# Five pairs of projections: a fixed order of their products, and the end of a head's attention one pair later

## The chip, the cores and the metric

The kernel runs on one core of one Trainium2 chip. The metric is the device time of one execution in microseconds, as a median of runs. The engines are named as the profile names them: PE is TensorE (matmuls; PEld its weight loads), DVE is VectorE, ACT is ScalarE, POOL is GpSimd, SP is SyncE, which here issues most of the DMAs. Each engine executes its instructions in the order in which the program has them.

## The reference

A decoder block for 512 tokens of width 2048. One projection gives two groups of heads: eight heads of 128 with compressed, selected and windowed attention (group A), and sixteen heads of 64 with a sliding window of 128 and a sink (group B). Each head's output is gated by a SiLU of a projected z. The output projection, the residual and an RMSNorm follow.

```python
def reference(x, w_in, ..., sinks, w_out, norm_g, final_g):
    h = _rmsnorm(x, norm_g[l])
    proj = h @ w_in[l]
    ...
    qb = _rope(_heads(qb, N_HEADS_B, HEAD_DIM_B)).reshape(B, S, N_KV_B, GROUP_B, HEAD_DIM_B)
    o_b = _banded_attention(qb, _rope(_heads(kb, N_KV_B, HEAD_DIM_B)), _heads(vb, N_KV_B, HEAD_DIM_B),
                            WIN_B, sink=sinks[l].reshape(N_KV_B, GROUP_B))
    y_b = o_b.reshape(B, S, WIDTH_B) * jax.nn.silu(zb)
    x = x + jnp.concatenate([y_a, y_b], axis=-1) @ w_out[l]
    return _rmsnorm(x, final_g)
```

## The kernel before

Everything is held in fp32, and each operand of a large matmul is split into a high and a low word: `unit` (L658) makes the high word by an ACT copy (L643) and the low word by a DVE subtraction (L644) of a 128x1024 quarter of weights, `raw`. A product's step is three matmuls, high by high, high by low and low by high (`mm3`, L126 to L129). There are three buffers for pairs of words.

The second group is worked through as eight "pairs" of 128 columns of q and 128 columns of z, h = 8 to 15. For h = 8 to 14 the function `pair` (L689) does not multiply the two 128-column blocks by x directly, but makes seven products of sums of quarters (a scheme of the Strassen kind) and combines them on DVE. Each product (`prod`, L668) is 8 steps, 24 matmuls of 128x128 by 128x256, into one half of a PSUM bank. A pair has two banks of 512 columns, `pa` and `pb`, out of a pool of two, so the next pair's `pb` is this pair's old `pa`. H0 and H1 are a bank's halves. In the order in which the code has them, the products are: "22" (pb H0), "p" (pa H0), "21" (pb H0, on top), "12" (pa H0, on top), "w" (pa H1), "u" (pb H1), "q" (pb H1, on top). Between them ACT copies halves out of the banks: 22's negated into `d` (L732), 21's into `zr` (L738), 12's into `qv` (`t1`, L747); DVE adds the rest with `plus` (L703).

The first pairs, h = 8 and 9, add quarters on DVE. In the five "wide" ones, h = 10 to 14, two quarters are summed while they are loaded: SP loads one (`load_quarter`, L686) and POOL issues a second load that accumulates onto it (L699). `tags` hands the buffers of a pair to the next in a rotated order.

The attention of the head whose q and z a pair has made (`attention`, from L880) is cut into jobs: s0 and s1 are scores and softmax of two parts (PE L900 and L901 into `spb`, DVE L904 to L908, ACT L909 to L918), k0 to k3 the transposes and values (PE L930 to L942, ACT L535 and L940), and `end` copies the result and gates it (`finish`, L512, which also stores it by a DMA). The loop at L947 hands these jobs as hooks to the next pair's products: `prod` calls them in the middle of the named product, and `behind_mm` (L663) keeps them behind the matmul issued last. Between these constraints, the order of the instructions on each engine is chosen by a scheduler, when the program is built, by its own estimate of times. After the loop, x is swapped in place for another copy (`swap_x`, L680), and `plain` makes the two 128-column blocks of h = 15 without the scheme.

## Time and profile before

| | |
|---|---|
| median of 3 runs | 826.99 us |
| lowest, highest | 824.44, 827.70 us |
| profiled execution | 826.69 us |
| its span, first to last instruction | 824.9 us |
| mean granted clock of PE | 0.999 |
| PE busy | 797.2 us |
| DVE busy | 685.4 us |

The span is the profiled execution's time from the first to the last instruction. The wide pairs lie between about 472 and 622 us of it. In rows in order of time, a number in brackets is the idle time of the engine just ahead of the instruction, with the instruction that the profile takes to have ended it. That name is inferred: where two instructions of an engine end close together, it can be the neighbour.

### The profile page before, as it was taken

What the parts mean: (1) busy time and instruction counts of PE and PEld (TensorE: products, weight loads), DVE (VectorE), ACT (ScalarE), POOL (GpSimd) and SP (SyncE); (2) the same over time, 40 slices, a digit from 0 to 9 for tenths busy, and PEclk for the clock granted to TensorE, in tenths of its full rate; (3) what the DMA queues carried; (4) which work ended last, traced back from release to release, by engine and by line L of the source; (5) the groups of instructions that cost most, each with busy time, mean ns of one, the idle gap of its engine ahead of it and who ended that gap; (6) DMA issues with size and microseconds to landing.
All of it is one profiled execution on the core that took longest, in us unless ns stands there. A gap on an engine that the chain in (4) does not pass through costs nothing.

```text
span 824.9 us, 15435 instructions
## 1 busy us (share of the span) xinstructions
PE 797.2 (97%) x5782; PEld 750.0 (91%) x5782; DVE 685.4 (83%) x1271; ACT 529.4 (64%) x1103; POOL 76.4 (9%) x69
## 2 busy tenths in 40 slices
PE   9999999999999999999999989999999999999996
PEld 8788898988999999999999989989888788999996
DVE  7869786865898989998898789989977588977895
ACT  6734456662677867868776568766866776553545
POOL 4500002012011011011010000000000000000000
PEclk9999999999999999999999999999999999999999
DMA  9655886899712314412321685656595336597835
GB/s 320 206 200 166 290 301 195 272 333 353 223 52 66 104 40 141 154 51 79 116 78 63 195 206 135 186 145 166 139 314 183 91 102 218 138 302 181 259 79 204
DMA packets 60954, 145.29 MB, mean 176 GB/s; under 512 B 6352, under 2 KB 19920, under 8 KB 60880
## 3 DMA queue, kind: packets, MB, share of 16 engines
q1 hardware_dynamic: 57424, 132.26, 48.7%
q0 software_dynamic: 3168, 11.54, 8.1%
q8 instruction: 45, 0.74, 0.4%
q10 hardware_dynamic: 288, 0.52, 0.2%
q14 instruction: 29, 0.24, 0.1%
HBM read 121.65 MB, written 20.55 MB: 172 GB/s over the span
## 4 chain that ended last, share of the span: by engine, by line
PE 75%; DVE 9%; ACT 6%; DMA 5%; issue 3%; POOL 1%; SPq 0%; DVEq 0%; ACTq 0%
PE pj L127 13%; PE pj L129 13%; PE pj L128 13%; PE oa L128 4%; PE oa L129 4%; PE oa L127 4%; PE bank L129 4%; PE bank L127 4%; PE bank L128 3%; PE sp L567 3%; DVE wlo L644 2%; DMA raw<-wq 2%; ACT whi L643 1%; DVE raw L703 1%; DMA xr<-xT 1%
## 5 line engine op out<-in xcount | busy, mean ns | idle before, releaser
L127 PE MATMUL pj<-xh,whi 128*128 128x256 f32 (+1 forms) x560 | 170.7, 305 | 8.7 <-DVE sums L907 2.6
L129 PE MATMUL pj<-xh,wlo 128*128 128x256 f32 (+1 forms) x560 | 170.1, 304 | 1.7 <-DVE wlo L644 1.7
L128 PE MATMUL pj<-xl,whi 128*128 128x256 f32 (+1 forms) x560 | 168.8, 301 | 0.0
L643 ACT ACTIVATE whi<-raw 128x1024 fp32r<-128x1024 f32 x98 | 103.0, 1054 | 55.3 <-PE pj L128 33.2
L644 DVE TENSOR_TENSOR wlo<-raw,whi 128x1024 fp32r<-128x1024 f32 x98 | 121.4, 1242 | 12.7 <-ACT whi L643 12.3
L127 PEld LDWEIGHTS pj<-xh,whi 128*128 128x128 f32 x560 | 105.4, 188 | 15.8 <-ACT whi L643 3.0
L129 PEld LDWEIGHTS pj<-xh,wlo 128*128 128x128 f32 x560 | 105.6, 189 | 7.0 <-DVE wlo L644 2.5
L128 PEld LDWEIGHTS pj<-xl,whi 128*128 128x128 f32 x560 | 105.4, 188 | 4.2
L97 DVE TENSOR_TENSOR wlo<-raw,whi 128x512 fp32r<-128x512 f32 (+2 forms) x74 | 81.3, 1104 | 33.5 <-ACT whi L96 33.0
L96 ACT ACTIVATE whi<-raw 128x1024 fp32r<-128x1024 f32 (+1 forms) x73 | 65.5, 901 | 53.1 <-PE pj L128 17.3
L127 PE MATMUL pj<-pu,whi 128*128 128x256 f32 x224 | 64.2, 287 | 2.9 <-DVE sums L908 1.5
L129 PE MATMUL pj<-pu,wlo 128*128 128x256 f32 x224 | 63.2, 282 | 0.5 <-DVE wlo L644 0.5
L128 PE MATMUL pj<-pu,whi 128*128 128x256 f32 x224 | 63.3, 283 | 0.0
L703 DVE TENSOR_TENSOR raw<-raw 128x1024 f32<-128x1024 f32 x46 | 59.1, 1285 | 0.2
L128 PE MATMUL oa<-wlo,xh 128*128 128x256 f32 (+1 forms) x168 | 50.9, 303 | 0.7 <-DVE wlo L1008 0.7
L127 PE MATMUL oa<-whi,xh 128*128 128x256 f32 (+1 forms) x168 | 50.4, 303 | 1.0 <-DVE sums L904 1.0
L129 PE MATMUL oa<-whi,xl 128*128 128x256 f32 (+1 forms) x168 | 50.3, 302 | 0.0
L127 PEld LDWEIGHTS pj<-pu,whi 128*128 128x128 f32 x224 | 42.3, 189 | 4.2 <-issue 1.6
L129 PEld LDWEIGHTS pj<-pu,wlo 128*128 128x128 f32 x224 | 42.3, 189 | 1.0 <-DVE wlo L644 0.9
L128 PEld LDWEIGHTS pj<-pu,whi 128*128 128x128 f32 x224 | 42.2, 188 | 0.0
L536 DVE TENSOR_TENSOR pl<-tp,ph 128x512 fp32r<-128x512 f32 x56 | 37.7, 683 | 4.9 <-ACT ph L535 4.8
L535 ACT ACTIVATE ph<-tp 128x512 fp32r<-128x512 f32 x56 | 32.1, 588 | 12.4 <-PE tp L930 8.4
(372 smaller groups left out, 2325.6 us busy)
## 6 DMA issues: line engine op xcount, KB each, us to landing
raw<-wq SPq DMA_DIRECT2D x65, 512.0 KB, 4.1
raw<-cw SPq DMA_DIRECT2D x16, 512.0 KB, 5.2
raw<-wos SPq DMA_DIRECT2D x15, 512.0 KB, 5.0
raw<-wq POOLq DMA_DIRECT2D x10, 512.0 KB, 5.5
rw<-wos SPq DMA_DIRECT2D x10, 512.0 KB, 5.2
xr<-xT SPq DMA_DIRECT2D x16, 256.0 KB, 5.1
raw<-w SPq DMA_DIRECT2D x8, 512.0 KB, 4.4
fd<-ft SPq DMA_DIRECT2D x4, 1024.0 KB, 6.0
```

What stands on the lines that cost most here:

```text
L96: last["hi"] = act.activation(hi[:, :width], rw[:, :width], AF.Copy).ins
L97: last["lo"] = dve.tensor_tensor(out=lo[:, :width], in0=rw[:, :width], in1=hi[:, :width].bitcast(F32), op=ALU.subtract).ins
L127: pe.matmul(ps, ah, bh, start=first, stop=False, skip_group_check=go_on)
L128: pe.matmul(ps, ah, bl, start=False, stop=False, skip_group_check=go_on)
L129: recent["mm"] = pe.matmul(ps, al, bh, start=False, stop=last, skip_group_check=go_on).ins
L535: act.activation(ph, tp, AF.Copy)
L536: dve.tensor_tensor(out=pl, in0=tp, in1=ph.bitcast(F32), op=ALU.subtract)
L567: pe.matmul(sp[:, a:b], qq[:, qs], kk[0][:, ko:ko + b - a], start=pi == 0, stop=pi == 2)
L643: act.activation(hi, src, AF.Copy)
L644: last["lo"] = dve.tensor_tensor(out=lo, in0=src, in1=hi.bitcast(F32), op=ALU.subtract).ins
L703: return dve.tensor_tensor(out=out, in0=a, in1=b, op=op).ins
```

## The change

`prod` gets a flag, `in_turn`, by which all matmuls of a product are kept behind the last matmul of the product before. The hooks are now called after the whole product has been written down, but still stand behind the matmul of its middle. `pair` keeps only h = 8 and 9. The five wide pairs get a function of their own, `wide_pair`, which prescribes the order 22, p, 21, 12, u, w, q: with u ahead of w, each product goes into the other bank than the one before it, and so does the next pair's 22, which follows q. The words of u are made ahead of those of w; `d` takes u first and w second. The buffers rotate in another way: the next pair's sum quarter takes the buffer of this pair's x3. In the loop, k0 moves from u to q, and k2, k3, k1 and `end` of a head no longer stand in q, or behind it, of the pair that does its scores, but in "p" of the pair after it; after the loop, in the plain product's third step.

```diff
-    def prod(bank, u, op, new, hooks=None):
-        for m in range(8):
...
-            if m == 3:
-                behind_mm((hooks or {}).get(op, ()))
+    def prod(bank, u, op, new, hooks=None, in_turn=False):
+        with ExitStack() as behind:
+            if in_turn:
+                behind.enter_context(tc.issue_after(last["prod"]))
+            for m in range(8):
...
+                if m == 3:
+                    mid = recent["mm"]
+        last["prod"] = recent["mm"]
+        recent["mm"] = mid
+        behind_mm((hooks or {}).get(op, ()))
+        recent["mm"] = last["prod"]
...
-            c1, c2, c5, c3, c4 = tags
-            tags[:] = c4, c1, c2, c3, c5
...
+    def wide_pair(h, hooks):
...
+        def do(bank, u, op, new):
+            prod(bank, u, op, new, hooks, True)
+
+        c1, c2, c5, c3, c4 = tags
+        tags[:] = c2, c1, c3, c4, c5
...
+        do(pb[:, H0], u0, "22", True)
+        act.activation(d, pb[:, H0], AF.Copy, scale=-1.0)
+        x3 = load(c3, 1)
+        do(pa[:, H0], u3, "p", True)
+        plus(d, d, pa[:, H0])
+        u2 = unit(x3)
+        do(pb[:, H0], u2, "21", False)
+        act.activation(zr[:, H1], pb[:, H0], AF.Copy)
+        u4 = unit(sm)
+        x4 = load(c4, 2, 3)
+        plus(sm, sm, x1)
+        plus(jj, d, zr[:, H1])
+        do(pa[:, H0], u4, "12", False)
+        act.activation(qv[:, H0], pa[:, H0], AF.Copy)
+        u5 = unit(sm)
+        plus(sm, sm, x3)
+        plus(jj, jj, qv[:, H0], ALU.subtract)
+        do(pb[:, H1], u5, "u", True)
+        plus(d, d, pb[:, H1])
+        u1 = unit(x4)
+        do(pa[:, H1], u1, "w", True)
+        plus(qv[:, H1], d, pa[:, H1])
...
+        u6 = unit(sm)
+        do(pb[:, H1], u6, "q", False)
+        plus(jj, jj, pb[:, H1])
+        plus(zr, zr, rstdb, ALU.mult)
...
-    held = None
+    held, tail = None, []
     for i in range(7):
-        hooks = {}
+        hooks = {"p": tail}
         if held:
             j, end, _ = held
-            hooks = {"12": [j["s0"]], "w": [j["s1"]], "u": [j["k0"]], "q": [j["k2"], j["k3"]], "end": [j["k1"], end]}
-        q2, st = pair(8 + i, (), hooks)
+            hooks.update({"12": [j["s0"]], "w": [j["s1"]], "q": [j["k0"]]})
+            tail = [j["k2"], j["k3"], j["k1"], end]
+        q2, st = wide_pair(8 + i, hooks) if i > 1 else pair(8 + i, (), hooks)
...
-    qp = plain(15, 0, {7: [j["s0"]], 11: [j["s1"]]})
+    qp = plain(15, 0, {2: tail, 7: [j["s0"]], 11: [j["s1"]]})
```

What this makes of the order on two engines is shown at three places. The first is PE where pair 12 begins, with the numbers of the buffers: `pj_6123` is the `pa` of pair 11 and `pj_6481` the `pb` of pair 12 (one bank), `xh`, `xl` are the words of x.

```order
L127 MATMUL pj_6123<-xh_108,whi_6289 128x256
L128 MATMUL pj_6123<-xl_109,whi_6289 128x256
L129 MATMUL pj_6123<-xh_108,wlo_6290 128x256
L127 MATMUL pj_6481<-xh_108,whi_6487 128x256
L128 MATMUL pj_6481<-xl_109,whi_6487 128x256
```

The next pair's 22 stood directly behind w of the same bank. In the changed kernel `pj_6084` is the `pb` of pair 11 and `pj_6441` the `pb` of pair 12, and `KH1`, `KL1` are operands of q:

```order
L127 MATMUL pj_6084<-KH1_123,whi_6393 128x256
L128 MATMUL pj_6084<-KL1_125,whi_6393 128x256
L129 MATMUL pj_6084<-KH1_123,wlo_6394 128x256
L127 MATMUL pj_6441<-xh_108,whi_6447 128x256
L128 MATMUL pj_6441<-xl_109,whi_6447 128x256
```

Now q, in the other bank, stands ahead of it.

The second place is ACT between the copies of 21 (L738) and 12 (L747) of pair 12; `whi` are splits into words, `ttb` with `sums` the softmax (L912 exponentials), `ph`, `pd` and `ob` copies for values.

```order
L738 ACTIVATE zr_6483<-pj_6481 128x256
L643 ACTIVATE whi_6705<-raw_6497 128x1024
L940 ACTIVATE pd_6439<-tp_6436 128x256
L535 ACTIVATE ph_6461<-tp_6456 128x512
L643 ACTIVATE whi_6764<-raw_6497 128x1024
L912 ACTIVATE ttb_6603,sums_6602<-ttb_6603,sums_6602 128x128
L949 ACTIVATE ob_6469<-opb_6365 64x512
L912 ACTIVATE ttb_6603,sums_6602<-ttb_6603,sums_6602 128x128
L909 ACTIVATE sums_6602<-sums_6602 128x4
L912 ACTIVATE ttb_6611,sums_6602<-ttb_6611,sums_6602 128x256 x2
L747 ACTIVATE t1_6482<-pj_6480 128x256
```

In the changed kernel the same two copies are L793 and L799, and L963 the exponentials:

```order
L643 ACTIVATE whi_6676<-raw_6585 128x1024
L793 ACTIVATE zr_6443<-pj_6441 128x256
L643 ACTIVATE whi_6750<-raw_6457 128x1024
L799 ACTIVATE t1_6442<-pj_6440 128x256
L535 ACTIVATE ph_6516<-tp_6511 128x512
L991 ACTIVATE pd_6527<-tp_6524 128x256
L643 ACTIVATE whi_6804<-raw_6802 128x1024
L963 ACTIVATE ttb_6615,sums_6614<-ttb_6615,sums_6614 128x128 x2
```

The two copies now stand one split apart, both ahead of the exponentials; before, that of 12 stood behind four of them.

The third place is ACT in pair 14 of the changed kernel (L969 are the softmax's normalisations, L819 the tanh of the gate).

```order
L643 ACTIVATE whi_7359<-raw_7171 128x1024
L643 ACTIVATE whi_7390<-raw_7299 128x1024
L969 ACTIVATE ttb_7062<-ttb_7062,sums_7061 128x256 x2
L969 ACTIVATE ttb_7070<-ttb_7070,sums_7061 128x256 x2
L819 ACTIVATE st_7151<-zr_6800 128x512
L799 ACTIVATE t1_7156<-pj_7154 128x256
L535 ACTIVATE ph_7230<-tp_7225 128x512
L991 ACTIVATE pd_7241<-tp_7238 128x256
L643 ACTIVATE whi_7464<-raw_7171 128x1024
L535 ACTIVATE ph_7250<-tp_7245 128x512
L793 ACTIVATE zr_7157<-pj_7155 128x256
L963 ACTIVATE ttb_7329,sums_7328<-ttb_7329,sums_7328 128x128 x2
```

Here the copy of 21 (L793) stands last, behind the copy of 12, a split and three copies for values.

## Rows read from the trace of the kernel before

**Rows 1.** Page part 1: engine, busy us, share of the span, instructions.
```profile
PE 797.2 (97%) x5782; PEld 750.0 (91%) x5782; DVE 685.4 (83%) x1271; ACT 529.4 (64%) x1103; POOL 76.4 (9%) x69
```

**Rows 2.** Table by stretches, one a pair; columns as in its second line.
```profile
core 0: us, PE busy (x) PEld busy (x) DVE busy (x) ACT busy (x) POOL busy (x), PEclk, DMA share, GB/s
528.91:557.35 28.44, 26.27 (x219) 25.32 (x219) 24.59 (x54) 21.48 (x50) 1.83 (x3) 1.00 0.59 145
557.35:583.58 26.23, 24.92 (x210) 24.44 (x211) 24.22 (x54) 18.04 (x41) 1.73 (x2) 1.00 0.61 165
583.58:611.80 28.22, 26.39 (x218) 25.40 (x218) 24.60 (x52) 20.89 (x49) 0.00 (x0) 1.00 0.71 210
```

**Rows 3.** PE in time: start us, us, instruction, idle before it, releaser.
```profile
479.78 0.36 PE L127 MATMUL pj<-pu,whi 128*128 128x256 f32 x1 [1.46 <-DVE sums L908]
...
484.64 0.38 PE L127 MATMUL pj<-xh,whi 128*128 128x256 f32 x1 [1.36 <-ACT dd L732]
...
502.57 0.39 PE L129 MATMUL pj<-xh,wlo 128*128 128x256 f32 x1 [0.24 <-DVE wlo L644]
...
528.91 0.36 PE L127 MATMUL pj<-xh,whi 128*128 128x256 f32 x1 [1.31 <-DVE sums L907]
...
542.23 0.38 PE L127 MATMUL pj<-pu,whi 128*128 128x256 f32 x1 [0.34 <-ACT whi L643]
...
551.99 0.39 PE L127 MATMUL pj<-xh,whi 128*128 128x256 f32 x1 [0.96 <-ACT t L747]
...
557.35 0.38 PE L127 MATMUL pj<-xh,whi 128*128 128x256 f32 x1 [0.87 <-DVE dd L703]
...
583.58 0.36 PE L127 MATMUL pj<-xh,whi 128*128 128x256 f32 x1 [1.31 <-DVE sums L907]
...
597.59 0.38 PE L127 MATMUL pj<-pu,whi 128*128 128x256 f32 x1 [0.47 <-ACT whi L643]
...
606.90 0.39 PE L127 MATMUL pj<-xh,whi 128*128 128x256 f32 x1 [0.95 <-ACT t L747]
...
611.80 0.50 PE L127 MATMUL pj<-xh,whi 128*128 128x512 f32 x1 [0.42 <-DVE dd L703]
```

**Rows 4.** VectorE in time, the additions that read w's half.
```profile
528.35 0.41 DVE L703 TENSOR_TENSOR dd<-dd,pj 128x256 f32<-128x256 f32 x1
...
556.88 0.41 DVE L703 TENSOR_TENSOR dd<-dd,pj 128x256 f32<-128x256 f32 x1
```

**Rows 5.** ScalarE in time, ahead of and at the copy of 12's half.
```profile
551.34 0.19 ACT L912 ACTIVATION_READ_ACCUMULATOR ttb<-ttb,sums 128x1 f32 x1
551.55 0.38 ACT L747 ACTIVATE t<-pj 128x256 f32<-128x256 f32 x1
```

**Rows 6.** Load chain of pair 10's sum quarter: SP, GpSimd and ScalarE in time.
```profile
472.45 0.61 SPq L686 DMA_DIRECT2D raw<-wq  x1
...
479.92 0.90 POOL L699 DMA_DIRECT2D raw<-wq  x1 [6.36 <-DMA raw<-wq]
...
485.48 1.06 ACT L643 ACTIVATE whi<-raw 128x1024 fp32r<-128x1024 f32 x1 [0.90 <-DMA raw<-wq]
```

**Rows 7.** ScalarE by line, 528.91 to 583.58: busy us, mean ns, idle before.
```profile
L643 ACT ACTIVATE whi<-raw 128x1024 fp32r<-128x1024 f32 x14 | 14.8, 1054 | 10.2 <-PE pj L128 9.4 <-ACT sums L909 0.8
...
L535 ACT ACTIVATE ph<-tp 128x512 fp32r<-128x512 f32 x6 | 3.5, 588 | 0.8 <-PE tp L930 0.8
...
L747 ACT ACTIVATE t<-pj 128x256 f32<-128x256 f32 x2 | 0.8, 384 | 0.0
```

**Rows 8.** Page part 6: DMA issues, count, KB each, median us to landing.
```profile
raw<-wq SPq DMA_DIRECT2D x65, 512.0 KB, 4.1
...
raw<-wq POOLq DMA_DIRECT2D x10, 512.0 KB, 5.5
```

**Rows 9.** DMA issues in 600 to 626, columns as in rows 8.
```profile
xh<-xd SPq DMA_DIRECT2D x2, 512.0 KB, 7.8
```

**Rows 10.** PE in time: w's last matmul, and the plain product's second half.
```profile
610.66 0.28 PE L129 MATMUL pj<-xh,wlo 128*128 128x256 f32 x1
...
621.35 0.40 PE L127 MATMUL pj<-xh,whi 128*128 128x512 f32 x1
```

More of the change, by code (lines that the diff above doesn't have):

```diff
@@ L666, in behind_mm @@
                 job()
[L668 to L674 removed]
+    def prod(bank, u, op, new, hooks=None, in_turn=False):
[3 more added lines that the diff above has]
+            for m in range(8):
+                cs = slice(m * P, m * P + P)
+                ah, al = xf[op, m]
+                mm3(bank, u[0][:, cs], u[1][:, cs], ah, al, new and m == 0, m == 7, not new)
+                if m == 3:
[4 more added lines that the diff above has]
+        recent["mm"] = last["prod"]
     def swap_x(source):
@@ L691, in pair, with load @@
         early = list(early)
-        wide = h > 9
-        def load(tag, quarter, other=None):
-            if early:
-                return early.pop(0)
-            t = load_quarter(src, tag, quarter)
-            if other is not None:
-                pool.dma_start(t, src[other], accum_op=ALU.add)
-            return t
+        def load(tag, quarter):
+            return early.pop(0) if early else load_quarter(src, tag, quarter)
         def plus(out, a, b, op=ALU.add):
             return dve.tensor_tensor(out=out, in0=a, in1=b, op=op).ins
-        if wide:
-            c1, c2, c5, c3, c4 = tags
-            tags[:] = c4, c1, c2, c3, c5
-        else:
-            c1, c2, c4, c3 = tags
-            tags[:] = (c4, c1, c3, c2) if h < 9 else (c4, c1, "raw4", c3, c2)
+        c1, c2, c4, c3 = tags
+        tags[:] = (c4, c1, c3, c2) if h < 9 else (c4, c1, "raw4", c3, c2)
         pa, pb = [psp.tile([P, S], F32, name="pj", tag="pj") for e in range(2)]
@@ L715, in pair @@
         d, jj = qv[:, H1], zr[:, H0]
-        if wide:
-            d = wb.tile([P, 256], F32, name="dd", tag="dd")
         x1 = load(c1, 3)
@@ L721, in pair @@
         u3 = unit(x2)
-        if wide:
-            sm = load(c5, 0, 2)
-        else:
-            sm = x2
-            x4 = load(c4, 2)
-            with ExitStack() as behind:
-                if "jj" in last:
-                    behind.enter_context(tc.issue_after(last["jj"]))
-                plus(x2, x2, x4)
+        sm = x2
+        x4 = load(c4, 2)
+        with ExitStack() as behind:
+            if "jj" in last:
+                behind.enter_context(tc.issue_after(last["jj"]))
+            plus(x2, x2, x4)
         prod(pb[:, H0], u0, "22", True, hooks)
@@ L740, in pair @@
         u4 = unit(sm)
-        if wide:
-            x4 = load(c4, 2, 3)
-        else:
-            plus(x4, x4, x1)
+        plus(x4, x4, x1)
         plus(sm, sm, x1)
@@ L764, in pair, with load, plus @@
         plus(jj, jj, pb[:, H1])
-        behind_mm((hooks or {}).get("end", ()))
         last["jj"] = plus(zr, zr, rstdb, ALU.mult)
+        st = wk.tile([P, S], F32, name="st", tag="st")
+        act.activation(st, zr, AF.Tanh, scale=0.5)
+        dve.scalar_tensor_tensor(out=st, in0=st, scalar=1.0, in1=zr, op0=ALU.add, op1=ALU.mult)
+        return qq, st
+    def wide_pair(h, hooks):
+        src = wq[h - FIRST]
+        def load(tag, quarter, other=None):
+            t = load_quarter(src, tag, quarter)
+            if other is not None:
+                pool.dma_start(t, src[other], accum_op=ALU.add)
+            return t
+        def plus(out, a, b, op=ALU.add):
+            return dve.tensor_tensor(out=out, in0=a, in1=b, op=op).ins
+        def do(bank, u, op, new):
+            prod(bank, u, op, new, hooks, True)
+        c1, c2, c5, c3, c4 = tags
+        tags[:] = c2, c1, c3, c4, c5
+        pa, pb = [psp.tile([P, S], F32, name="pj", tag="pj") for e in range(2)]
+        qv = wk.tile([P, S], F32, name="t1", tag="t1", bufs=1)
+        zr = wk.tile([P, S], F32, name="zr", tag="xr", bufs=1)
+        d, jj = wb.tile([P, 256], F32, name="dd", tag="dd"), zr[:, H0]
+        x1 = load(c1, 3)
+        u0 = unit(x1)
+        x2 = load(c2, 0)
+        u3 = unit(x2)
+        sm = load(c5, 0, 2)
+        do(pb[:, H0], u0, "22", True)
[20 more added lines that the diff above has]
+        plus(qv[:, H1], d, pa[:, H1])
+        t2 = wk.tile([P, S], F32, name="t2", tag="t2", bufs=1)
+        for a, b in ((0, 64), (64, 0)):
+            dve.tensor_tensor(out=t2[a:a + 64], in0=qv[b:b + 64], in1=sinA[b:b + 64], op=ALU.mult)
+        dve.tensor_tensor(out=qv, in0=qv, in1=cosA, op=ALU.mult)
+        dve.tensor_tensor(out=qv, in0=qv, in1=t2, op=ALU.add)
+        qq = qb_split(qv)
+        u6 = unit(sm)
+        do(pb[:, H1], u6, "q", False)
+        plus(jj, jj, pb[:, H1])
+        plus(zr, zr, rstdb, ALU.mult)
```

3 lines of the change are left out of this document (removed).

## Prediction

> **What bounds the kernel now.** I read the engines' shares first: PE is busy 797.2 us and DVE 685.4 us [rows 1], in a span of 824.9 us. PE is the engine that is hardly ever idle, so only what removes an idle stretch of PE can shorten the run by itself; nothing in this change removes matmuls. The second view is the table by stretches, one row for each of three wide pairs [rows 2]. The reader is to see two things there: PE is idle for 1.3 to 2.2 us in each pair (28.44 less 26.27, 26.23 less 24.92, 28.22 less 26.39), and DVE is busy 24.2 to 24.6 us in each, that is, at most 1.8 us below PE. ACT, with 18.0 to 21.5 us, has more room on the whole, but it works in order as well. So the gain has a floor that is near: if PE loses its gaps, a pair takes some 25 us, and DVE fills nearly all of that.
>
> The third view is PE in order of time, and from it the rows with an idle stretch ahead of them, from the first of pair 10 to the first of the plain product that follows pair 14 [rows 3]. These are all that are over 0.2 us: eleven, in sum 9.69 us. They fall into four kinds. (a) The first product of the next pair, "22", stands directly behind "w", whose half lies in the same bank: 1.31, 0.87 and 1.31 us, and 0.42 us where the plain product stands there, 3.91 us together. The releaser's name "sums L907" is that of the neighbour; what really ends just ahead is the DVE addition of the half that w has written (it starts at 528.35 and lasts 0.41 us, PE goes on at 528.91; at 556.88 with 0.41 us, PE at 557.35) [rows 4]. (b) "w" waits for ACT's copy of "12" out of the other half of its own bank, 0.96 and 0.95 us; the copy started at 551.55 and lasted 0.38 us, w started at 551.99 [rows 5]. (c) Words that come late: 0.24, 0.34 and 0.47 us. (d) The two of pair 10, 1.46 and 1.36 us.
>
> **The change part by part.** *q between w and the next 22.* PE then has the 24 matmuls of q, and 8 score products, ahead of the 22 that waits for DVE's reading of w. A matmul takes about 24.92 us / 210 = 0.119 us of PE's time [rows 2], so q alone covers 2.8 us against waits of 0.87 to 1.31 us. All of kind (a) goes: -3.91 us. What is late next there is q's own words: their raw sum is the last of three additions on DVE, and the old order had q even later, without a wait, so I put that at 0; if the cover failed the 22's wait would come back, up to 1.31 us a pair.
>
> *12, scores, u, w.* PE's order of these three is as before; what moves is ACT's. The copy of 12 now stands ahead of the next softmax's exponentials and not behind them, so (b) goes: -1.91 us. (c) goes with it, since u's words are now made ahead of w's: -1.05 us. Together what can be had behind pair 10 is 6.87 us.
>
> *Pair 10.* Its gaps I leave in the sum. The words of its 12 come at the end of a serial chain: the load issued at 472.45, the accumulating load behind it at 479.92, ACT's split at 485.48 [rows 6]. 12 cannot start earlier than this, and the chain is not touched. If PE were sooner at 12 by 2.82 us it would wait there. Between 0 and 0.5 us may be had; I take 0.
>
> *What the new order adds.* u goes into the bank into which 21 went, and both orders need 21's copy by ACT first. Before, that copy had long been done. Now it is queued on ACT behind the splits of two further words and four normalisations. A split takes 1.05 us, a copy of a half 0.38 us and a copy of transposed weights 0.59 us [rows 7]. Following ACT's queue with these through pairs 11 to 13, the copy ends 0.1 to 0.4 us after PE is ready for u: 0.25 us each, +0.75 us. In pair 14 it is worse: behind the copy of 12 stand a copy of transposed weights (0.59), a smaller one (0.38 as a half), a split (1.05), another copy of weights (0.59) and only then the copy for u (0.38), 3.0 us, while PE has only 8 score products and 11 transposes and values, 19 times 0.119 us = 2.3 us at most, part of them ahead of ACT's start. The wait there is between 0 (the queue runs ahead) and 2.5 us (the normalisations ahead of it run late as well). The nearest row is the wait for ACT's copy in the same pair before, 0.95 us [rows 3]; I take 1.0 us. In pairs 12 and 13 the copy of 22's half stands behind the two copies that make the rotated queries, and 21 waits for it: 0 to 0.7 us, I take 0.35 each, +0.7 us. Sum of the additions: +2.45 us.
>
> A rule speaks against counting the neighbours alone. By the rows the wait is for the bank, not for the bytes: w writes one half and waits for the copy of the other [rows 3, 5]. The Trainium skill, "PSUM — Partial Sum Buffer", section "PSUM bank collisions raise a hardware error", says that a different address in the same bank and quadrant still collides, and asks for semaphores by bank. By it u waits for ACT's copy of 21 though a whole product lies between them, and w for the copy of 12: a prescribed order of products does not take that dependence away, only the time of ACT's queue does. The rows agree with it. If ACT kept its old place for these copies the two waits would be gone, and the sum would be 2.45 us lower.
>
> *The tail of the head before, in "p" of the next pair.* The same instructions, about 5 us later on PE and off the path: values, additions and one store. On SP the store and on ACT the copies stand behind the next pair's first splits; who waits for them is the output stage after 650 us. Cost 0; bounds -0.3 to +0.5 us a pair, by the copies' 0.38 to 0.59 us [rows 7], if they stand ahead of a split that PE needs.
>
> *Buffers.* The sum quarter's accumulating load now takes the buffer of x3 and is issued only when the last raw addition has read it, late in the pair. From there to ACT's split of it I count some 16 us. A load lands after 4.1 us and an accumulating one after 5.5 us [rows 8], 9.6 us serially, so it is hidden; pair 10's chain took 13.0 us (472.45 to 485.48) [rows 6] and would be hidden as well. Cost 0, slack 3 to 6 us.
>
> *The end of the stretch.* The swap of x into the odd places goes out when w has ended, as before. The loads of it land after 7.8 us [rows 9]. Before, the second half of the plain product that needs it began 10.7 us after w's last matmul (621.35 against 610.66) [rows 10], since q lay inside it; now q lies ahead of all of it, and the need comes some 9.9 us after w. 0 to 1 us, I take 0.
>
> The sum is -6.87 + 2.45 = -4.4 us. The profiled execution took 826.69 us (1.8 us around its span), which is 0.3 us under the median of 826.99 us; the difference is applied to the median: **822.6 us**.
>
> **Rivals.** *All waits go.* ACT runs ahead of its queue and the additions are 0: -6.87 us, 820.1 us. For it: ACT is idle some 7 to 8 us in a pair [rows 2]. Against: it must be idle at the right time, and its order is fixed.
>
> *The wait moves.* With PE's order fixed, one late word stops everything behind it, where before PE's queue had an attention piece or another product in between. DVE needs 24.6 us of the 25 that are left, and ACT's queue holds copies that PE waits for. If each of four pairs loses 1.5 us in this way (kinds a and b came to 1.3 to 1.8 us a pair), then -6.87 + 6 is about -1: 826 us. DVE's share speaks for it.
>
> The Trainium skill, "Perfetto Trace Analysis", section "Identifying the Most-Contended Engine", has matmul busy time as a poor measure and the weight loads' as a better one. The weight loads are busy 24.44 us where matmuls show 24.92 [rows 2]; by that PE has half a microsecond more room in a pair, and DVE would be the bound by 24.2 against 24.4, nearly a tie, which speaks for this rival a little.
>
> *Slower: the sum quarter comes late.* One mechanism: its buffer is free later, so two serial transfers start later. It decides when the two together exceed 16 us. Were both twice as long as now (8.2 + 11.0 = 19.2 us), each of four pairs would wait 3.2 us: -4.4 + 12.8 gives 835 us. Against: the longest chain seen is 13.0 us.
>
> *The change does not do what it says.* If PE's effective order were much as before, the time stays: 827 us. The order written down in the program speaks against it.
>
> **How the numbers follow.** Chances: forecast 0.44 (821 to 824.3), all waits go 0.20 (818 to 821), the wait moves 0.22 (824.3 to 828), sum quarter late 0.09 (over 831), no effect 0.05. About 0.5% is what a measurement of this kernel can tell from no change, that is 4.1 us: faster means under 822.9. The forecast's own range lies on both sides of that: 0.27 under, 0.17 within. Faster 0.27 + 0.20 = 0.47; same 0.17 + 0.22 + 0.04 = 0.43; slower 0.09 + 0.01 = 0.10. The range leaves out the sum quarter's case and the outer end of "all waits go", and takes in the bounds of the unknown costs: 818.0 to 828.0.
>
> **What would show it.** Right: no idle stretch ahead of a pair's 22; none ahead of w; small ones, released by ACT's copy, ahead of u, the largest in pair 14; the pairs 11 to 14 some 25.2 us long; pair 10 as before. Wrong: idle of PE behind DVE's splits in every pair (the wait moved), a wait of ACT for the accumulating load ahead of 12 (sum quarter late), or a pause in the middle of the plain product (swap late).

## The result, and the profile after

The change makes the kernel slower: 833.58 us against 828.87 us (medians of 7 runs each, 4.7 us apart). The ratio on record, over all runs, is 1.0069 [1.0041 to 1.0096], by which the loss is some 5.7 us. The forecast was 822.6 us. One execution of i1 below, 839.17 us, is over 1.5% above the fastest of its kernel and is left out of its median.

| | before | after |
|---|---|---|
| profiled execution, us | 826.69 | 831.98 |
| its span, us | 824.9 | 830.2 |
| granted clock of TensorE, mean | 0.999 | 0.994 |
| PE idle in the span, us | 27.7 | 30.0 |

The first part of the page, as in [rows 1], and the shares of the chain that ended last:

```profile
PE 800.2 (96%) x5782; PEld 752.1 (91%) x5782; DVE 683.7 (82%) x1271; ACT 529.6 (64%) x1103; POOL 76.9 (9%) x69
...
PE 71%; DVE 11%; ACT 8%; DMA 6%; issue 3%; SPq 0%; POOL 0%; DVEq 0%; ACTq 0%
```

In these two profiles the loss has two parts, and the first line shows both. The same 5782 matmuls are busy 3.0 us longer (800.2 against 797.2), and PE is idle 2.3 us more (830.2 less 800.2 against 824.9 less 797.2). The chain's share of PE, 75% before, is 71%: more of it runs through waits on other engines.

PE in order of time, the rows with a longer idle stretch ahead of them, from pair 10 to the output stage (start us, us, instruction, idle before it and its releaser; in a block of columns of that stage that is made by seven products the first is called p, the second 22):

```profile
487.74 0.39 PE L127 MATMUL pj<-xh,whi 128*128 128x256 f32 x1 [1.93 <-ACT whi L643]
...
513.45 0.38 PE L127 MATMUL pj<-xh,whi 128*128 128x256 f32 x1 [0.90 <-ACT dd L787]
...
540.49 0.38 PE L127 MATMUL pj<-xh,whi 128*128 128x256 f32 x1 [1.59 <-ACT dd L787]
...
566.64 0.38 PE L127 MATMUL pj<-xh,whi 128*128 128x256 f32 x1 [0.22 <-ACT dd L787]
...
599.11 0.36 PE L951 MATMUL spb<-VH,qs 128*128 128x256 f32 x1 [1.54 <-DMA qs<-qlo]
...
603.51 0.38 PE L127 MATMUL pj<-pu,whi 128*128 128x256 f32 x1 [1.05 <-ACT zr L793]
...
702.63 0.39 PE L127 MATMUL oa<-whi,xh 128*128 128x256 f32 x1 [2.63 <-ACT whi L1059]
...
731.90 0.38 PE L127 MATMUL oa<-whi,xh 128*128 128x256 f32 x1 [1.15 <-ACT whi L1059]
```

Set beside [rows 3], none of the eleven gaps is left in its place: no row ahead of a pair's 22, none ahead of w. In their stead stand fewer and longer ones: 12 of pair 10 (1.93), 21 of pairs 11 to 13 (0.90, 1.59, 0.22), the scores in pair 14 (1.54), u of pair 14 (1.05), and two in the output stage (2.63, 1.15), where the longest before was 0.69.

The table by stretches, columns as in [rows 2]: pairs 11, 12 and 13, and then two short stretches directly behind a wait, in pair 10 and in the output stage.

```profile
506.29:532.64 26.35, 25.45 (x216) 24.91 (x215) 24.49 (x54) 19.72 (x45) 1.73 (x2) 1.00 0.67 170
532.64:559.72 27.08, 25.49 (x217) 24.95 (x216) 24.04 (x55) 21.11 (x49) 1.74 (x2) 1.00 0.65 161
559.72:585.20 25.48, 25.26 (x217) 24.64 (x216) 23.93 (x53) 19.67 (x45) 1.74 (x2) 1.00 0.60 156
488.40:491.80 3.40, 2.93 (x15) 2.87 (x15) 3.18 (x5) 3.19 (x7) 0.00 (x0) 0.51 0.23 35
703.50:706.80 3.30, 3.30 (x17) 3.30 (x17) 3.30 (x6) 2.22 (x4) 0.00 (x0) 0.50 0.53 169
```

The pairs are 25.5 to 27.1 us long, PE idle 0.2 to 1.6 us in each. In the two short stretches the granted clock is 0.51 and 0.50, the lower of the two levels (1.2 GHz): in the second, matmuls start 0.21 us apart (703.61 to 706.81), right behind it 0.11 us. Each stretch costs at most 1.7 us, its length by one less the clock; what is called lost by the clock below is counted so, and is a bound from above, since PE also waits in part of some stretches. In the profile of before the clock is full from the first pair to the last microseconds. Its mean, 0.999, is the highest that any execution of that kernel shows; the 22 beside h0 below have 0.993 to 0.999, so a part of this difference is the choice of the execution.

Set against before, the 5.3 us of span come out so. PE is 1.3 us late at 457 us already, in front of the change (the idle there varied by more than a microsecond between profiles, and is no effect of it). From there to the first product of the output stage, at 655.34 us (654.12 before), it wins 1.6 us of idle time (9.0 against 10.65 us) and loses 1.7 us by the clock behind the wait of pair 10: nothing is won. From there to the end it takes 4.1 us more, with 2.6 us more of waits and 1.7 us by the clock in the stretch shown, and that stage's code isn't touched by the change.

**The output stage.** What the scheduler did there is seen on ScalarE, VectorE and SyncE, at the end of head 15, three answers in this order:

```profile
686.33 0.60 ACT L1000 ACTIVATE ob<-opb 64x512 f32<-64x512 f32 x1 [4.50 <-PE opb L988]
687.48 1.06 ACT L1059 ACTIVATE whi<-raw 128x1024 fp32r<-128x1024 f32 x1 [0.55 <-PE pj L129]
688.57 0.59 ACT L1000 ACTIVATE ob<-opb 64x512 f32<-64x512 f32 x1
...
686.96 0.68 DVE L1001 TENSOR_TENSOR ob<-opb,ob 64x512 f32<-64x512 f32 x1 [3.87 <-ACT ob L1000]
688.57 1.23 DVE L1060 TENSOR_TENSOR wlo<-raw,whi 128x1024 fp32r<-128x1024 f32 x1 [0.93 <-ACT whi L1059]
689.83 0.68 DVE L1001 TENSOR_TENSOR ob<-opb,ob 64x512 f32<-64x512 f32 x1
690.55 0.69 DVE L514 SCALAR_TENSOR_TENSOR y<-ob,st 128x512 f32<-128x512 f32 x1
...
692.80 1.31 SPq L1228 DMA_DIRECT2D rw<-wos  x2
```

The same place in the kernel before (ScalarE, VectorE, SyncE, and the first matmul of 22 on PE):

```profile
684.37 0.60 ACT L949 ACTIVATE ob<-opb 64x512 f32<-64x512 f32 x1 [3.29 <-PE opb L937]
685.72 0.59 ACT L949 ACTIVATE ob<-opb 64x512 f32<-64x512 f32 x1 [0.75 <-DVE ob L950]
...
687.06 0.69 DVE L514 SCALAR_TENSOR_TENSOR y<-ob,st 128x512 f32<-128x512 f32 x1
...
689.27 1.22 SPq L1176 DMA_DIRECT2D rw<-wos  x2
...
699.72 0.28 PE L127 MATMUL oa<-whi,xh 128*128 128x256 f32 x1
```

A split of the output stage's first words (L1059, L1060) now stands between the two halves of head 15's result, `ob`; before, the two stood together. Of the 3.49 us by which `y` is later (690.55 against 687.06), 1.96 are there already at the first `ob`, 1.53 come from the split between. The loads of `rw`, the words of 22, which go out when `y` is made, are issued 3.53 us later. PE is ready for their product at 700.00, only 0.28 us later than before, and waits. The chain of waits from there (start, us, what) has the load's whole time on it, ahead of ACT's split L1059 and PE's 22:

```profile
692.80 8.63 DMA rw<-wos
```

**Pair 14's scores.** The chain ahead of the wait of 1.54 us shows what stands between `t`, the rotated query, and the transfer that the scores need:

```profile
588.67 0.56 DVE t L812
589.23 0.60 DVE pl L536
...
590.53 0.68 DVE ob L1001
591.25 0.27 DVE wlo L644
...
592.39 0.42 DVE dd L770
592.80 0.60 DVE st L514
593.40 0.60 DVE qlo L925
...
594.60 4.38 DMA qs<-qlo
```

`qlo` is the subtraction that the transfer waits for; it starts 4.1 us behind the end of `t` here. `ob` and `st` are the end of the head before, which the change moved into this pair's p, 1.3 us of it. Not all of that counts, since `qlo` also needs ACT's copies `qs`, and these stand behind ACT's copy of 22 and end at 592.2 us. In the kernel before, VectorE has `qlo` 1.9 us behind `t`, and no `ob` or `st` of a head between them:

```profile
587.29 0.69 DVE L760 TENSOR_TENSOR t<-t,t 128x512 f32<-128x512 f32 x1
...
589.91 0.68 DVE L874 TENSOR_TENSOR qlo<-t,qs 128x512 fp32r<-128x512 f32 x1
```

### The profile page after: what moved, and what is told of

The parts are those of the page before. It is cut to its first block, busy times and chain, and to the rows that moved or that the text cites. A ratio compares the mean times of both kernels' runs of the same rounds, so it can differ in the third digit from the quotient of the medians.

```text
span 830.2 us, 15410 instructions
## 1 busy us (share of the span) xinstructions
PE 800.2 (96%) x5782; PEld 752.1 (91%) x5782; DVE 683.7 (82%) x1271; ACT 529.6 (64%) x1103; POOL 76.9 (9%) x69
## 4 chain that ended last, share of the span: by engine, by line
PE 71%; DVE 11%; ACT 8%; DMA 6%; issue 3%; SPq 0%; POOL 0%; DVEq 0%; ACTq 0%
PE pj L127 12%; PE pj L129 12%; PE pj L128 12%; PE bank L129 4%; PE bank L127 4%; PE bank L128 4%; PE oa L128 4%; PE oa L129 4%; PE oa L127 3%; PE sp L567 3%; DMA raw<-wq 2%; DMA xr<-xT 2%; DVE wlo L644 2%; ACT ttb L963 1%; PE tp L605 1%
## 5 line engine op out<-in xcount | busy, mean ns | idle before, releaser
L644 DVE TENSOR_TENSOR wlo<-raw,whi 128x1024 fp32r<-128x1024 f32 x98 | 121.2, 1242 | 11.7 <-ACT whi L643 10.6
L704 DVE TENSOR_TENSOR raw<-raw 128x1024 f32<-128x1024 f32 x36 | 46.9, 1303 | 0.2
L128 PE MATMUL bank<-wlo,xh 128*128 128x256 f32 (+1 forms) x128 | 40.0, 315 | 0.0
```

Source lines behind the costliest of these rows:

```text
L128: pe.matmul(ps, ah, bl, start=False, stop=False, skip_group_check=go_on)
L644: last["lo"] = dve.tensor_tensor(out=lo, in0=src, in1=hi.bitcast(F32), op=ALU.subtract).ins
L704: return dve.tensor_tensor(out=out, in0=a, in1=b, op=op).ins
```

## Experiments

Each was run five rounds against the kernel before, on the same chip; ratios are to that. h0, h1, i1 to i3, f1, f3 and e6 ran on one chip; e1 to e4 and the g runs ran on others, with no changed kernel beside them. Two theories were put against each other at first: the loss comes from single places (the output stage's order, pair 10's late words and the half clock behind the waits), or the wait moves wherever one is taken away, since DVE and ACT set the pace.

**The output stage: head 15's end first.** The first splits of the output stage are put behind `y` of head 15: in the changed kernel (e3), and once more (h1) beside a repetition of the changed kernel (h0). The edit comes back in g2 and i2 below.

```
-        u3 = [halves(load(raw(), 0, g)) for g in range(2)]
+        raw3 = [load(raw(), 0, g) for g in range(2)]
+        with tc.issue_after(last["y"]), tc.issue_after(last["ob"]):
+            u3 = [halves(r) for r in raw3]
```

> The changed kernel with one thing more: in the output stage the two splits of the first weights (L1059) are kept behind the end of head 15 on ACT and DVE, so that no split lies between the two copies of its result any more. Theory (the output stage pays): head 15 ends some 1.9 us sooner (691.25 to about 689.3), the loads into its freed room start sooner, PE's idle of 2.63 us at 702.63 shrinks to 0 to 0.7 us and the stretch at half clock behind it (703.5 to 706.8) goes: 2.5 to 4.3 us less than the changed kernel, a ratio to the kernel before of 1.002 to 1.004. Rival (the fixed order of the products itself costs): the time of the changed kernel stays, 1.006 to 1.008, since its pairs are untouched.

> The changed kernel once more, as the partner of h1_end_first_again on one chip. 1.006 to 1.008. In the profile: the wait ahead of 12 of pair 10 is between 1.9 and 3.7 us (it hangs on two loads in series, and four traces with the same order there showed 1.9, 2.2, 3.5 and 3.7 us), the wait ahead of the output stage's first 22 some 2.6 us, with the clock at half behind both.

> The kernel of e3_end_first once more, beside the changed kernel on the same chip. Theory (two separate costs): 2.5 to 4.5 us less than the changed kernel, as g2_end_later_first against g1_end_later, 1.001 to 1.004; e3_end_first's profile was one of its two slowest executions. Rival (the later wait of w for its two serial loads takes the gain back in this kernel): within 1.5 us of the changed kernel, with a wait of 3 us or more ahead of w's low words at about 730.

e3: 832.18 us, 1.0073 [1.0043, 1.0102]: no gain to be seen, with no changed kernel beside it on that chip. In its profile the wait ahead of the output stage's first 22 was gone, but 12 of pair 10 waited 3.66 us, pair 14's scores 2.67 and a w of the output stage 4.36 us, each with a stretch of half clock behind it. Side by side it is another picture: h0 832.41 us, 1.0051 [1.0028, 1.0075]; h1 830.05 us, 1.0019 [1.0000, 1.0039]. The edit is worth 2.4 us, with intervals that overlap; up to the output stage the two profiles have the same order on PE, ACT and DVE. In h1's profile, PE in order of time, the wait at the first 22 is gone, e3's 4.36 us is 1.50, and pair 10's wait is there still:

```profile
489.44 0.58 PE L127 MATMUL pj<-xh,whi 128*128 128x256 f32 x1 [3.79 <-ACT whi L643]
...
729.26 0.38 PE L128 MATMUL oa<-wlo,xh 128*128 128x256 f32 x1 [1.50 <-DVE wlo L1060]
```

**Pair 10: the narrow form, and the end of a head still later.** f3 gives pair 10 the form of pairs 8 and 9; g3 does the same in the kernel before; g1 has f3's edit and moves a head's `end` from "p" to "q", behind the queries' split; g2 is g1 with head 15's end first.

```
-        q2, st = wide_pair(8 + i, hooks) if i > 1 else pair(8 + i, (), hooks)
+        q2, st = wide_pair(8 + i, hooks) if i > 2 else pair(8 + i, (), hooks)
...
-            hooks.update({"12": [j["s0"]], "w": [j["s1"]], "q": [j["k0"]]})
-            tail = [j["k2"], j["k3"], j["k1"], end]
+            hooks.update({"12": [j["s0"]], "w": [j["s1"]], "q": ends + [j["k0"]]})
+            ends = [lambda end=end: behind_split(end)]
+            tail = [j["k2"], j["k3"], j["k1"]]
```

The first two lines are f3's (and, with `wide = h > 10`, g3's), the rest is g1's.

> The changed kernel with pair 10 made by the function for pairs 8 and 9: its quarters are added on DVE and no accumulating load stands ahead of its 12; the wide form begins with pair 11. Theory (pair 10's gain was turned into one wait for two serial loads, with half the clock behind it): the wait of 1.9 to 3.7 us ahead of 12 and the low stretch behind it (1.7 to 3.4 us lost) go; two more raw additions on DVE (2.4 us) and pair 10's own gaps of the old kind (about 2.7 us) come in: 1 to 4 us less than the changed kernel, 1.002 to 1.006. Rival (the cost lies in the output stage and in pair 14): no change, 1.006 to 1.008.

> The kernel before with pair 10 in the form of pairs 8 and 9. Theory (pair 10's loads became a cost only since the change brings PE there sooner): no gain here, two more raw additions on DVE against the 2.8 us of gaps in pair 10: 0.998 to 1.003. Rival (the narrow form of pair 10 is better by itself, and f3_narrow10's gain has nothing to do with the change): 4 to 5 us less, 0.994 to 0.996.

> The changed kernel with pair 10 in the form of pairs 8 and 9 (as f3_narrow10), and with the end of a head moved from p of a pair to its q, behind the split of that pair's queries, so that the queries of the next scores go out first. The scheduler's order in the output stage is the bad one here: a split of weights lies between the two copies of head 15's result. Theory (two separate costs, pair 10 and the output stage): 1 to 2 us are won ahead of pair 14's scores, and the waits of about 2.6 us at the output stage's first 22 with the low clock behind it are there: 1.004 to 1.006, slower than f3_narrow10 (1.0019). Rival (pair 10 alone is the cost): 1.000 to 1.002, the output stage's order makes no difference.

> g1_end_later with one thing changed: the first splits of the output stage are kept behind the end of head 15, as in e3_end_first, so that the two copies of its result stand together. Up to there the order of every engine is the same as in g1_end_later. Theory (the output stage costs by its own order): 2.5 to 4.5 us less than g1_end_later, 0.999 to 1.002. Rival (pair 10 alone): as g1_end_later, within 1 us.

f3: 828.54 us, 1.0019 [0.9994, 1.0043], most of the loss gone; but its output stage also fell back into the old order, so it doesn't say which of the two did it. g3: 1.0011 [0.9998, 1.0025]: in the kernel before the narrow form alone gains nothing, so f3's gain is not the form's by itself. g1: 848.98 us, 1.0252 [1.0227, 1.0276], far from both theories; u waits for ACT's copy of 21 in each of pairs 12 to 14 (2.34, 2.33, 2.33 us), with half clock behind each. g2: 844.49 us, 1.0204 [1.0181, 1.0226]. g1 and g2 have one order up to the output stage and disjoint intervals: 4.5 us is the price of its order there, as the theory had it, though not the level. ScalarE in time shows it, first g1, then g2:

```profile
702.15 0.60 ACT L1000 ACTIVATE ob<-opb 64x512 f32<-64x512 f32 x1 [4.50 <-PE opb L988]
703.30 1.06 ACT L1064 ACTIVATE whi<-raw 128x1024 fp32r<-128x1024 f32 x1 [0.55 <-PE pj L129]
704.38 0.59 ACT L1000 ACTIVATE ob<-opb 64x512 f32<-64x512 f32 x1
```

```profile
703.96 0.60 ACT L1000 ACTIVATE ob<-opb 64x512 f32<-64x512 f32 x1 [4.49 <-PE opb L988]
705.31 0.59 ACT L1000 ACTIVATE ob<-opb 64x512 f32<-64x512 f32 x1 [0.75 <-DVE ob L1001]
```

**Pair 10: its sum quarter loaded early.** The buffer of the sum quarter is exchanged with another in pair 10: in e4 with that of x3, in i1 with that of x4; i2 is i1 with head 15's end first; i3 is i2 with the scores of pair 14 behind u's middle and q's words behind the copy of 21.

```
         c1, c2, c5, c3, c4 = tags
+        if h == 10:
+            c5, c4 = c4, c5
...
+        with tc.issue_after(copy21):
+            u6 = unit(sm)
...
-            hooks.update({"12": [j["s0"]], "w": [j["s1"]], "q": [j["k0"]]})
+            hooks.update({"12" if i < 6 else "u": [j["s0"]], "w": [j["s1"]], "q": [j["k0"]]})
```

The first edit is i1's (e4 has c3 in place of c4), the others are i3's.

> The changed kernel, with the buffers of x3 and of the sum quarter exchanged in pair 10 alone, so that the sum quarter's two serial loads start some 7 us sooner there and x3's single load takes the late place. Theory (in pair 10 the gain became one long wait for the sum quarter, and the clock fell behind it): the idle of 1.93 and 0.47 us at 487.74 and 488.94 goes and with it the stretch at half clock (488.4 to 491.8, worth 1.7 us): 3 to 4 us less than the changed kernel, a ratio of 1.002 to 1.004. Rival (the wait is only moved to 21 of pair 10, whose words now come late, or to a later copy): 0 to 1 us less, 1.006 to 1.007.

> The changed kernel with the buffers of the sum quarter and of x4 exchanged in pair 10 alone: the sum quarter's two serial loads go out early, and x4's two, needed only by w, take the late place. (e4_sum_early exchanged it with x3, whose product comes sooner, and the wait moved there.) The output stage keeps the bad order. Theory A (pair 10's wait and the low clock behind it are a cost of their own): the 1.9 to 3.8 us ahead of 12 go, 2 to 4 us less than the changed kernel, 1.001 to 1.003. Theory B (the output stage holds the whole loss, what PE gains at pair 10 waits for ACT, DVE and the queries' transfers later): 0 to 1 us less, 1.004 to 1.007.

> i1_sum_early with the output stage's first splits behind the end of head 15 (as e3_end_first). Theory A: both costs gone, 0.996 to 0.999, under the kernel before. Theory B: as e3_end_first on its own, 1.001 to 1.003. Against i1_sum_early both expect 2.4 to 4.5 us less, the price of the output stage's order.

> i2_sum_early_end_first, with the scores of pair 14 behind the middle of u there instead of behind 12, and q's words kept behind ACT's copy of 21. In the profiles the scores of pair 14 wait 1.5 to 2.5 us for the transfer of the queries, and u 1.0 us for the copy of 21. Theory (these two waits and the clock behind them are the rest of the loss): they go, 2 to 4 us less than i2_sum_early_end_first, 0.993 to 0.996. Rival (the pairs are paced by ACT and DVE, so what is won there is lost ahead of the plain product or of head 14's scores): within 1 us of i2_sum_early_end_first.

e4: 837.62 us, 1.0119 [1.0091, 1.0146], worse: the buffer that the sum quarter no longer waits for is missing to x3, and now 21 waits 5.99 us, with a stretch of half clock of 10.2 us that begins in the wait (at most 5.1 us lost). i1: 831.94 us, 1.0043 [1.0019, 1.0068]; i2: 829.69 us, 1.0009 [0.9989, 1.0029]; i3: 828.31 us, 1.0003 [0.9981, 1.0024]. PE in time, i1:

```profile
597.38 0.36 PE L953 MATMUL spb<-VH,qs 128*128 128x256 f32 x1 [2.18 <-DMA qs<-qlo]
...
601.76 0.58 PE L127 MATMUL pj<-pu,whi 128*128 128x256 f32 x1 [2.06 <-ACT zr L795]
```

Pair 10's wait is gone, but pair 14 waits 4.24 us in two places (2.59 in the first profile of the changed kernel, 3.28 in h0's), with the half clock there (at most 3.4 us lost): by this profile pair 14 takes what pair 10 gives, and the time is that of h0 within the error. i1 to i2 is 2.3 us, the output stage's order once more (the order up to there is one). i2 to i3 is 1.4 us, between what the two theories gave and within the error; the scheduler also moved other instructions, from pair 12 on, so it is not the price of pair 14's scores alone. i3's profile in time:

```profile
485.14 0.38 PE L127 MATMUL pj<-xh,whi 128*128 128x256 f32 x1 [1.71 <-ACT dd L789]
...
512.19 0.38 PE L127 MATMUL pj<-xh,whi 128*128 128x256 f32 x1 [1.27 <-ACT dd L789]
...
591.42 0.39 PE L127 MATMUL pj<-xh,whi 128*128 128x256 f32 x1 [1.08 <-ACT dd L789]
...
598.66 0.33 PE L984 MATMUL tp<-ident,ttb 128*128 128x128 f32 x1 [1.04 <-ACT ttb L972]
...
699.40 0.39 PE L127 MATMUL oa<-whi,xh 128*128 128x256 f32 x1 [2.19 <-ACT whi L1062]
```

With pair 10 and pair 14 mended the time is that of before, and not less. The waits over 0.15 us from 458 us on have new names and the old sum, 12.0 us. But they stand elsewhere, as two stretches show: from the wait in front of the wide pairs to the output stage's first product, and from there to the end; first before, then i3, columns as in [rows 2]:

```profile
455.93:654.12 198.19, 187.35 (x1446) 176.79 (x1446) 168.16 (x376) 138.57 (x321) 9.99 (x12) 1.00 0.65 182
654.12:824.91 170.79, 162.19 (x1210) 154.11 (x1210) 136.17 (x182) 95.08 (x151) 9.57 (x11) 0.99 0.61 179
457.86:652.70 194.84, 186.96 (x1445) 176.44 (x1446) 166.80 (x376) 138.26 (x321) 10.03 (x12) 1.00 0.66 185
652.70:826.64 173.94, 162.12 (x1210) 153.54 (x1210) 136.66 (x182) 95.11 (x151) 9.59 (x11) 0.98 0.60 176
```

In i3 the pairs take 3.3 us less than before, at full clock, against 4.4 us forecast, and the output stage takes 3.1 us more. There the third place isn't mended after all: the two `ob` copies stand together, but on PE the last of head 15's values stands 158 matmuls behind the stage's first product (146 before, 144 in the changed kernel), `y` comes 35.8 us behind the stage's first product (32.9 before, 35.2 in the changed kernel, 33.7 in i2), and 22 waits 2.19 us for `rw` with half clock behind it. So here the pairs' gain is real and is lost behind them. This is one execution each: the two profiles of the changed kernel, with one order, take 198.1 and 201.9 us (h0) in the first stretch, the second with 5.1 us of half clock.

**Parts of the change undone.** e1 puts a head's tail back where it was (k2 and k3 in q, k1 and `end` behind it); e2 takes the prescription off, so that only the order of the code is left; e6 puts the queries' split behind ACT's copy of the next 22.

```
-            hooks.update({"12": [j["s0"]], "w": [j["s1"]], "q": [j["k0"]]})
-            tail = [j["k2"], j["k3"], j["k1"], end]
+            hooks.update({"12": [j["s0"]], "w": [j["s1"]], "u": [j["k0"]], "q": [j["k2"], j["k3"]], "end": [j["k1"], end]})
...
-            prod(bank, u, op, new, hooks, True)
+            prod(bank, u, op, new, hooks, False)
...
-        act.activation(d, pb[:, H0], AF.Copy, scale=-1.0)
+        copy = act.activation(d, pb[:, H0], AF.Copy, scale=-1.0).ins
+        for q2, old in pending:
+            with tc.issue_after(copy):
+                q2.extend(qb_split(old))
```

> The changed kernel with the jobs of a head's attention back in their old places (k0 in u, k2 and k3 in q, k1 and end behind q), products in turn and buffers as in the change. Theory (the output stage pays, through the order that the scheduler made there): the two copies of head 15's result stand together again here, so PE's idle near 702 and the half clock behind it go, pair 10's wait stays: 2.5 to 4.3 us less than the changed kernel, 1.002 to 1.004. Rival (moving the tail costs by itself, in the pairs): 5 us or more less, 1.001 or under, with the waits ahead of 21 and of pair 14's scores gone. Rival (the fixed order costs): as the changed kernel, 1.006 to 1.008.

> The changed kernel without the constraint that keeps each product behind the one before; code order, buffers and hooks as in the change. Theory (the output stage pays): the order on PE hardly differs in the pairs, and the two copies of head 15's result stand together, so it runs 2.5 to 4.3 us faster than the changed kernel, 1.002 to 1.004. Rival (the fixed order of products costs): idle ahead of 21, of 12 and of u goes with the constraint and the time falls to that of the kernel before or under, 1.000 or less.

> The changed kernel with the split of the rotated queries (two ACT copies and one DVE subtraction) kept behind ACT's copy of the next pair's 22 in pairs 11 to 14. Theory for the pairs (21 waits for that copy because it is queued behind the queries' copies): the idle of 0.90, 1.59 and 0.22 us ahead of 21 falls by 1.5 to 2 us; if no long wait is touched, the clock stays and the time falls by that much, 1.004 to 1.005. Rival (21's wait has another source, words or DVE, or the queries then come late for the scores): no gain or a loss, 1.006 to 1.010.

e1: 832.89 us, 1.0064 [1.0045, 1.0083]. With the tail in its old place the output stage has its old order and no wait at the first 22, and takes 170.9 us, as before (170.8); pair 14's scores wait 0.50 us instead of 1.54: the tail was behind both. Yet the time hardly moves: 12 of pair 10 waits 2.21 us with two stretches of half clock behind it (at most 3.4 us lost), the stretch of the pairs takes 201.9 us as in h0, and a w of the output stage waits 1.88. e2: 833.77 us, 1.0078 [1.0059, 1.0098]: the order on all three engines changes: pair 10's 22 begins ahead of pair 9's q again, and the waits ahead of 12 of pair 10 and of the first 22 of the output stage are gone from the profile, but pair 14's transposes wait 3.77 us, with at most 3.4 us lost by the clock. Freeing the order gains nothing; what the constraint costs by itself it doesn't say. e6: 834.27 us, 1.0063 [1.0036, 1.0089]: 21 waits 0.90, 0.46 and 0 us in pairs 11 to 13 (0.90, 1.59, 0.22 before this edit), but in pair 14 the scores 1.93 and u 2.66 us (1.54 and 1.05). The wait moved.

**Filling the waits.** f1 puts 38 more matmuls, whose results nobody reads, into the waits of pair 10 (12), pair 14 (6) and the output stage (14 and 6), to hold the clock. The piece of pair 10:

```
         do(pb[:, H0], u2, "21", False)
+        if h == 10:
+            fill(12, u2, "21")
```

> The changed kernel with 38 matmuls more, whose results nobody reads, on PE ahead of the four places at which its traces show the long waits: 12 ahead of 12 of pair 10, 6 ahead of the scores in pair 14, 14 ahead of 22 and 6 ahead of w of the output stage's first column block. They are 4.5 us of work (38 at 0.119 us) that PE does while it waits. Theory (the cost is the clock: the change gathers PE's idle time into single long waits, and behind these PE runs at half clock for 3.4 or 6.8 us): with work in the waits the low stretches go, the mean granted clock rises from 0.988 to 0.994 to the 0.995 to 0.998 of the kernel before, and though work is added the time falls by 2 to 5 us, to a ratio of 1.001 to 1.004. Rival (the waits themselves cost, the clock is a side effect of little weight): no gain, or a loss of up to 4.5 us where the work isn't covered: 1.007 to 1.012.

836.98 us, 1.0103 [1.0074, 1.0131]: no gain, and by the medians a loss against the changed kernel, whose ratios are 1.0051 and 1.0069 (the intervals overlap). Its page, part 1, and the stretch of pair 10 in the table by stretches:

```profile
PE 800.5 (96%) x5820; PEld 750.8 (90%) x5820; DVE 684.4 (82%) x1271; ACT 529.1 (63%) x1103; POOL 76.9 (9%) x69
```

```profile
488.40:491.80 3.40, 2.67 (x20) 2.18 (x19) 2.28 (x2) 3.39 (x7) 0.00 (x0) 1.00 0.03 10
```

In this execution the clock was held in the pairs; in the output stage one stretch is left, behind the wait of 1.95 us. Less some 4.5 us for the 38 (by 0.118 us each), the kernel's own matmuls are busy 796.0 us, 1.2 us less than before the change. But PE is idle 33.8 us (834.3 less 800.5): pair 14's scores wait 2.31 us, a later piece 2.24, and one of the output stage 1.95. And this execution is among the better ones by its clock, 0.996: the six have 0.994 in the mean, at most 5.1 us of their span, where h0 has 0.992 and 6.6 us. So as a rule the fillers held little of the clock, and moved the order besides; what the half clock costs by itself this run doesn't show.

## Why the prediction was wrong

**Kinds (a), (b) and (c): right, and not enough.** The 6.87 us of gaps went as worked out: none stands ahead of 22 or w in the profile after. One failing step was the additions set against them. The sum left 6.2 us of waits from 457 us to the output stage (10.6 less 4.4); 9.0 came. Ahead of 21 it was 2.0 us more than forecast, and pair 14's scores and the values behind them took 2.1 us that the sum had at nothing. In i3 it was 7.5 us, without low clock, and there most of the forecast came true in the pairs (3.3 of 4.4 us). The rival "the wait moves" was the nearest: it was priced at 1.5 us in each of four pairs, 826 us, and it named ACT's queue, which is what 21 and u waited for. Its sign, PE idle behind DVE's splits in every pair, did not come.

**Pair 10, "I take 0".** PE does wait there, as written: the gain of the pair is given back in one wait instead of two. Mis-sized is what hangs on it. The wait was 1.93 to 3.79 us with this order (the loads' landing varies), and behind it stood half clock in all of these profiles but h0's, at most 1.7 to 3.4 us. The sum had no term for that, here or anywhere else. The slack of 3 to 6 us given for the sum quarter did not hold in pair 10: its two loads went out as late as before (473.27 and 481.00 against [rows 6]) while PE came earlier. Still, taking the wait away (i1) moved the median by 0.5 us only.

**21 behind the queries' copies: undersized.** 0.35 us in each of pairs 12 and 13 was forecast; 1.59 and 0.22 came, 1.8 against 0.7 us. Pair 11's 0.90 has another source, which the sum left out: there the copy of 22 (513.01) stands ahead of the queries' copies (513.29), behind four exponentials, four normalisations and a split, and the 0.90 stayed when e6 moved the queries' copies. **u: oversized, then right.** None in pairs 11 to 13 (0.75 forecast), 1.05 in pair 14 (1.0 forecast). The rule of the Trainium skill weighed there ("PSUM — Partial Sum Buffer", "PSUM bank collisions raise a hardware error") agrees with these rows: in pair 14, and in g1 by 2.3 us a pair, u waits for the copy of another half of its bank.

**The tail, "who waits for them is the output stage after 650 us. Cost 0": the step that failed most.** It has two sides. On DVE the tail stands ahead of the queries' split, and pair 14's scores wait (1.54 us; 0.50 with the tail put back, e1). And the last head's end reached the output stage in another order, by which the scheduler put a split into the middle of it; `y` and the loads behind it were 3.5 us late. That is 2.4 us (h0 to h1), 2.3 (i1 to i2) and 4.5 (g1 to g2), with one order up to there in each of the three. In i3 the stage's order turned out bad in another way. The sum ended at the plain product, and nothing behind it was priced, although the order of the instructions there could be read before the run.

**"Slower: the sum quarter comes late"** was the wrong mechanism for the right sign. It asked for more than 16 us of two serial loads in the pairs behind 10, and none of these waits for its sum quarter. In pair 10 the chain took 13.4 us, and up to 15.8 us (h1), but there it was PE that came earlier, not the loads that went out later.

**What adds up, and what stays open.** On one chip the changed kernel stands at 1.0051 and i3 at 1.0003, 4.0 us apart. Shown of this is the price of the output stage's order (2.3 to 2.4 us). Pair 14's scores (1.4) and pair 10's load (0.5 to 0.7) are each within the error, and both edits moved the order in other pairs as well. The rest of the missing gain is, by i3's profile, in the output stage again. That DVE, busy 24 of the 25.5 us that a pair without waits takes, bounds what the pairs can gain is argued, not shown.

A second count, over all executions, points to the clock. The 11 of h0 have a mean granted clock of 0.992, at most 6.6 us of their span; the 22 of the kernel before beside them 0.997, at most 2.4 us. The difference, 4.2 us, is about the whole loss there (4.4 us between the means). In i3 it is 4.3 against 2.7 us, so that kernel would be shorter by up to 1.6 us but for the clock. The prediction's sum had no such term. How much of each wait's price is the wait and how much the half clock stays open: the low stretches begin in or behind the waits, f1 held the clock in one execution and lost more by other waits, and e1 has neither the bad output order nor the long wait for scores and is no faster (0.9 us of that, in its profile, are from in front of the change).

## What to carry to other kernels

When the bounding engine's gaps are to be removed, price the new waits in every engine's queue, and follow the gain to the end of the program: what one stage wins can be lost in the next. Moving "free" work in one stage moves the scheduler's order in the stages behind it: compare the order to the end of the program, above all around loads that wait for a result. And a few long waits can cost more than many short ones.

## What was not expected of the hardware

TensorE's granted clock fell to its lower level in or behind single waits, in a kernel in which PE is busy 96% of the span. From 380 to 820 us every stretch of low clock in these profiles has a wait of 1.88 us or more ahead of it or reaching into it; the profile of before, whose longest wait there is 1.46 us, has none. The reverse doesn't hold: a wait of 2.21 us (h0, pair 10) and one of 2.86 us (i1, output stage) had full clock behind them. What tells these apart the rows don't show. The stretches were 3.4, 6.8 or 10.2 us long, at most 1.7, 3.4 and 5.1 us lost. Most executions of the kernel before have a mean clock under the 0.999 of its profile too; what stands ahead of their low stretches wasn't traced.
